# Two squares ahead of the first SiLU, one store per query part, late w_out pieces and the quotient at other blocks, the prompt's sums on VectorE

## The chip, the core and the metric

The kernel runs on one core of a Trainium2 chip. A core has TensorE (PE, the matrix engine; its weight loads are listed as PEld), VectorE (DVE), ScalarE (ACT), GpSimd (POOL) and SyncE (SP). Each engine works through its own instructions in order and waits on semaphores for the others. SP computes nothing; here it issues most of the DMAs, and ACT issues the rest. A DMA that has to wait for something holds up all that stands behind it in the same queue. The metric is the time of one execution on the device in microseconds (us).

## What is computed

One layer of a diffusion step: 128 context ("prompt") tokens and 1024 latent tokens, width 1024, with one combined input projection for two groups of heads, A (mixer 0, all latent keys) and B (mixer 1, a window of 128 to each side, with a sink logit). Cut to what matters:

```python
shift, scale, gate = modulation(cond, w_mod, b_mod)          # silu(cond) @ w_mod + b_mod
h = rmsnorm(x, norm_gain) * (1.0 + scale) + shift
q_a, k_a, v_a, g_a, q_b, k_b, v_b, g_b = project(h, w_in, qn_a, kn_a, qn_b, kn_b)
# latent tokens: q and k through apply_rope
o_a = softmax(q_a @ [k_ctx, k_lat].T / 8) @ [v_ctx, v_lat]
o_b = softmax([sink, q_b @ [k_ctx, k_band].T / 8])[1:] @ [v_ctx, v_band]
x = x + gate * (concat(o_a * silu(g_a), o_b * silu(g_b)) @ w_out)
# the prompt attends to its own keys alone; its k and v are outputs too
```

Everything is float32. To keep the precision, the kernel splits an operand into a high and a low part and adds two or three matmuls.

## The kernel before, in words

There are nine tiles of 128 tokens: `t` = 0 is the prompt, 1 to 8 are the latent tiles. The order of the instructions on every engine is that of the program text (`in_order`). A step is put off with `later(n, f)`: `f` runs `n` ticks on, and `block` (L276) ticks twice per projection block, the attention loop (L1309) once per slot.

*Start (L342 to L567).* SP loads latent tiles 1 to 4 and then, piece by piece, the modulation weights `wm` and the first columns of `w_in`. ACT loads the condition vectors `colt` and takes their SiLU (L375). `norm(t)` (L413) then takes the squares of a tile with their sum on ACT, the mean on POOL (L419), and a power of -0.5 on POOL (L421); `scaled` (L410) multiplies the tile on DVE. `turned` (L427) transposes a block of it on TensorE. Between the four transposes TensorE runs `warm(n)` (L461), matmuls whose results are not used, by the list `WARM`. After the fourth transpose come the modulation of the first block (`modulate_rows`, L387) and the matmuls of the first gates.

*Queries (L615 to L726).* For each mixer `m` and tile `t`, TensorE projects the queries; `query` (L650) normalizes, rotates and transposes them. `turned` (L683) copies the high part out of PSUM on ACT (L689), `low` (L693) takes the low part on DVE (L694), and `put` (L697) stores each part to DRAM in two DMAs, one for each half of the partitions, into `q_dram`, an array of 128 rows x 1024. The last three tiles of mixer 1 (`LAST_QUERIES`) are stored by SP, the others by ACT. The buffers of a part are two. After the queries SP loads the key tables `kcos` and `ksin` (L777), into memory that the queries used, and the keys are made (`key`, L819; `put_keys`, L779; transposes at L791, low parts at L809).

*Attention (L1131 to L1329).* The work is cut into 36 units (t, m, g), g being a half of the heads; the four prompt units come last. A unit of mixer 0 has 9 key blocks (1 for the prompt), one of mixer 1 three or four, and each block is a slot. In a slot TensorE makes the scores of this block (L1164 and L1165 for mixer 0, L1159 for mixer 1), and three slots later (`LAG`) it multiplies with the values (L1185 to L1188). The scores L1165 need `qb`, loaded by SP (L927) and completed by DVE (L942). `u_load` (L898) loads a unit's queries. After a unit's last block its end is spread over the next slots by `END_AT` = (1, 4, 6, 9): `inverse` on ACT (L1197 or L1199), `gated` on DVE and POOL (L1209, L1211), `parts` (L1221, L1223), and the output projection (L1256). The accumulator `pv` has two buffers, so the values of unit i + 2 wait for `gated` of unit i.

For mixer 1, `weight_items` (L951) makes the softmax: `ex` (L1001), its exponential (L1012), the sum (L1015) and its reciprocal (L1018). The prompt's four heads are then multiplied by it on DVE (L1021).

Five pieces of `w_out` (11 to 15) are loaded late, at the slots that `WO_LATE` gives, into a tag of two buffers (`yt`), and are split three slots later (L1078 on ACT, L1079 on POOL). The last piece of the gates is turned into a SiLU by way of exponentials and a logarithm (`put_quotient`, L302), at ticks that `QUOTIENT_AT` sets.

Of the kernel before, what the change touches and what calls it, by code (L numbers as in the profile page):

```python
# [49 lines left out]
QUOTIENT_AT = 9  # L50
# [3 lines left out]
WO_LATE = {12: 18, 13: 19, 11: 20, 14: 30, 15: 31}  # L54
# [7 lines left out]
WARM = (7, 4, 5, 4, 2, 8)  # L62
# [10 lines left out]
END_AT = (1, 4, 6, 9)  # L73
PROMPT_END = (2, 4, 5, 7)
# [7 lines left out]
LAST_QUERIES = ((1, 7), (1, 8), (1, 0))  # L82
CACHE_AT = 8
# [30 lines left out]
def hybrid_step(ctx, tc, x_prompt, x_sample, cache_k_a, cache_v_a, cache_k_b, cache_v_b,  # L114
# [9 lines left out]
    q_dram = [[dram.tile([P, 1024], F32, name=f"qd{t}_{m}") for m in range(2)] for t in range(NT)]  # L124
# [218 lines left out]
    with tc.tile_pool(name="st", bufs=2, side="right") as st:  # L343
# [6 lines left out]
        nc.scalar.dma_start(colt, cols)  # L350
        st.tile([P, 16], F32, name="pad3", bufs=1)
# [32 lines left out]
        nc.vector.tensor_copy(sil32[:, :, 0:2], sil2)  # L384
# [28 lines left out]
        def norm(t, now_=True):  # L413
            xm = xn[t]
            sq = st.tile([P, D], BF16, tag="sq", name=f"sq{t}", bufs=1)
            ss = st.tile([P, 1], F32, tag="ss", name=f"ss{t}")
            nc.scalar.activation(sq, xm, AF.Square, accum_out=ss)
            ms = st.tile([P, 1], F32, tag="ms", name=f"msx{t}")
            nc.gpsimd.tensor_scalar(ms, ss, 1.0 / D, EPS, op0=ALU.mult, op1=ALU.add)  # L419
            r = st.tile([P, 1], F32, tag="rs", name=f"rsx{t}")  # L420
            nc.gpsimd.tensor_tensor(r, ms, mhalf[:, 0:1], op=ALU.pow)  # L421
            if now_:
                scaled(t, r)
            else:
                rx[t] = r
# [59 lines left out]
        for j in range(KT + 2):  # L485
            if j == 0:
                px = bank_tr("px0_1")
                for i in range(4):
                    norm(1 + i)
                    warm(WARM[i])  # L490
                    turned(px[:, P * i : P * i + P], 0, 1 + i)
                modulate_rows(0)
                W_GA.split()
                warm(WARM[4])
                modulate(0)
                modulated(px, 0, 1, 4, 0)
                warm(WARM[5])
                continue
# [3 lines left out]
            if j == 1:  # L502
                load_wm(3)
                norm(5, False)
# [15 lines left out]
            if j == 1:  # L520
# [3 lines left out]
                norm(6, False)  # L524
# [27 lines left out]
            if X_FROM < j <= X_FROM + 3:  # L552
                norm(rest[j - X_FROM - 1], False)
# [61 lines left out]
    with tc.tile_pool(name="qt", bufs=2, side="right") as qt:  # L615
# [34 lines left out]
        def query(pq, m, t, tabs, n=1):  # L650
# [32 lines left out]
            def turned():  # L683
# [7 lines left out]
                (later if (m, t) not in ((1, 0), (1, 5)) else at_once)(1, lambda: low(ptq, qo))  # L691

            def low(ptq, qo):  # L693
                nc.vector.tensor_tensor(qo[1], ptq, qo[0], op=ALU.subtract)  # L694
                (later if (m, t) != (1, 0) else at_once)(1, lambda: put(qo[1], 1))

            def put(part, i):  # L697
                for g in range(2):
                    (nc.sync if (m, t) in LAST_QUERIES else nc.scalar).dma_start(q_dram[t][m][64 * i : 64 * i + 64, 512 * g : 512 * g + 512],
                                       part[64 * g : 64 * g + 64].bitcast(F32))  # L700
# [197 lines left out]
    def u_load(i):  # L898
# [3 lines left out]
        nc.sync.dma_start(qt_.bitcast(F32), q_dram[t][m][:, 512 * g : 512 * g + 512])  # L902
        qtile[i] = qt_

    def max_items(i):
# [19 lines left out]
        def finish():  # L925
            qb_ = qp.tile([68, 512], F32R, tag="qb", name=f"qb{i}", bufs=2)
            nc.sync.dma_start(qb_[0:64, :].bitcast(F32), q_dram[t][m][0:64, 512 * g : 512 * g + 512])  # L927
# [23 lines left out]
    def weight_items(i):  # L951
# [48 lines left out]
        def finish():  # L1000
            nc.gpsimd.tensor_tensor(v["ex"], v["nm"], sink[:, 4 * g : 4 * g + 4], op=ALU.add)  # L1001
# [12 lines left out]
        def total():  # L1014
            nc.gpsimd.tensor_tensor(v["sum"], v["sum"], v["ex"], op=ALU.add)  # L1015
# [162 lines left out]
    def values(i, b, last, blk, ph, pl):  # L1178
# [46 lines left out]
        ends = END_AT if t else PROMPT_END  # L1225
# [167 lines left out]
```

## Time and profile before

| | us |
|---|---|
| three runs | 720.32, 720.82, 721.16 (median 720.82) |
| the profiled execution | 720.69 |
| its span, first to last instruction | 718.9 |
| TensorE busy | 698.7 (97%) |
| DVE, ACT, POOL busy | 454.2, 413.9, 338.3 |
| mean granted TensorE clock | 0.995 |

In a row of the timeline the columns are start, length, engine, line, operation, output <- inputs, shapes and count, and in brackets the engine's idle time before it and what ended it; SPq and ACTq are DMA issues. A row of waits is: who waited, for what, us in total, how many times, the longest. A row of windows has the stretch, its length, the busy time of PE, PEld, DVE, ACT and POOL (with the number of instructions), the granted TensorE clock, the share of the DMA engines and GB/s. A row of a line or tile gives the shortest, median and longest duration in ns, and the first and last start in us.

### The profile page before, as it was taken

What the parts mean: (1) busy time and instruction counts of PE and PEld (TensorE: products, weight loads), DVE (VectorE), ACT (ScalarE), POOL (GpSimd) and SP (SyncE); (2) the same over time, 40 slices, a digit from 0 to 9 for tenths busy, and PEclk for the clock granted to TensorE, in tenths of its full rate; (3) what the DMA queues carried; (4) which work ended last, traced back from release to release, by engine and by line L of the source; (5) the groups of instructions that cost most, each with busy time, mean ns of one, the idle gap of its engine ahead of it and who ended that gap; (6) DMA issues with size and microseconds to landing.
All of it is one profiled execution on the core that took longest, in us unless ns stands there. A gap on an engine that the chain in (4) does not pass through costs nothing.

```text
span 718.9 us, 10656 instructions
## 1 busy us (share of the span) xinstructions
PE 698.7 (97%) x3530; PEld 559.1 (78%) x3530; DVE 454.2 (63%) x1002; ACT 413.9 (58%) x835; POOL 338.3 (47%) x357
## 2 busy tenths in 40 slices
PE   6999999999999999999899999999999999999987
PEld 2678988877787889976688888888888888887765
DVE  3575247866757853567566677567676775676552
ACT  4546411412323441188678877887788778877850
POOL 3466023232313330255767554755575557556660
PEclk9999999999999999999999999999999999999999
DMA  9951273348445025422132122121221221222223
GB/s 350 385 195 68 107 297 76 84 127 263 107 93 149 2 73 185 148 66 86 52 103 63 48 67 89 45 81 58 83 73 39 72 82 46 81 69 71 89 81 118
DMA packets 53304, 78.57 MB, mean 109 GB/s; under 512 B 6585, under 2 KB 25465, under 8 KB 52353
## 3 DMA queue, kind: packets, MB, share of 16 engines
q1 hardware_dynamic: 45888, 67.70, 28.7%
q10 hardware_dynamic: 7360, 10.19, 5.3%
q8 instruction: 28, 0.46, 0.3%
q14 instruction: 28, 0.22, 0.1%
HBM read 58.69 MB, written 19.18 MB: 108 GB/s over the span
## 4 chain that ended last, share of the span: by engine, by line
PE 87%; DVE 5%; issue 2%; POOL 1%; ACT 1%; DMA 1%; SPq 1%; ACTq 0%; DVEq 0%; POOLq 0%
PE po L1256 13%; PE pv L1185 6%; PE pv L1188 6%; PE pmx L922 5%; PE st L1164 5%; PE st L1165 5%; PE pv L1187 5%; PE pq L257 4%; PE pq L258 4%; PE pq L259 4%; PE st L1159 4%; PE pg L271 3%; PE pg L272 3%; PE pg L267 3%; PE sn L979 2%; PE sn L980 2%
## 5 line engine op out<-in xcount | busy, mean ns | idle before, releaser
L1175 POOL TENSOR_TENSOR pl<-pe,ph 128x512 fp32r<-128x512 f32 x130 | 167.6, 1291 | 150.3 <-DVE nm L983 65.9
L923 DVE TENSOR_REDUCE mx<-pmx 128x1 f32<-128x384 f32 x192 | 101.0, 552 | 59.9 <-PE pmx L922 58.7
L1167 ACT ACTIVATE pe<-st 128x512 f32<-128x512 f32 x146 | 86.9, 596 | 29.7 <-PE st L1165 28.9
L1171 ACT CAST ph<-pe 128x512 fp32r<-128x512 f32 x146 | 90.6, 620 | 4.8
L1185 PE MATMUL pv<-ph,v_hi 128*128 128x512 f32 x208 | 83.0, 399 | 2.3 <-DVE spare L1209 2.3
L1188 PE MATMUL pv<-pl,v_hi 128*128 128x512 f32 x208 | 82.8, 398 | 0.0
L1256 PE MATMUL po<-wo,ogh 128*128 128x512 f32 x216 | 74.0, 399 | 0.2 <-DVE yt L1265 0.2
L182 POOL TENSOR_TENSOR rs_q<-ms_q,mhalf 128x8 f32<-128x8 f32 x18 | 34.8, 1931 | 81.8 <-DVE ms_q L180 81.8
L983 DVE CUSTOM_DVE_ANT_0 sn<-sn,mask,nsink 128x512 f32<-128x512 f32 (+1 forms) x64 | 46.4, 725 | 40.5 <-PE sn L980 37.6
L922 PE MATMUL pmx<-kha,qt 128*128 128x384 f32 x192 | 61.5, 367 | 0.3 <-DVE mx L923 0.2
L1165 PE MATMUL st<-qb,kla 68*128 68x512 f32 x144 | 57.6, 400 | 2.8 <-DMA qb<-qd 2.8
L1164 PE MATMUL st<-qt,kha 128*128 128x512 f32 x144 | 57.7, 401 | 0.9 <-DVE pl L1161 0.9
L1187 PE MATMUL pv<-ph,v_lo 128*64 128x512 f32 x146 | 57.8, 396 | 0.0
L1188 PEld LDWEIGHTS pv<-pl,v_hi 128*128 128x128 f32 x208 | 39.6, 190 | 17.1 <-POOL pl L1175 0.7
L969 ACT ACTIVATE pen<-sn,nm 128x512 f32<-128x512 f32 (+2 forms) x72 | 45.1, 628 | 6.1 <-DVE nm L996 2.7
L1185 PEld LDWEIGHTS pv<-ph,v_hi 128*128 128x128 f32 x208 | 39.5, 190 | 10.4 <-ACT ogh L1221 2.1
L1160 ACT CAST ph<-st 128x512 fp32r<-128x512 f32 x62 | 36.4, 587 | 18.2 <-PE st L1159 17.6
L1256 PEld LDWEIGHTS po<-wo,ogh 128*128 128x128 f32 x216 | 40.6, 191 | 7.2 <-DVE yt L1265 0.6
L1161 DVE TENSOR_TENSOR pl<-st,ph 128x512 fp32r<-128x512 f32 x62 | 42.4, 685 | 4.7 <-ACT ph L1160 4.1
L1256 PE MATMUL po<-wo,ogl 128*128 128x512 f32 x108 | 42.8, 397 | 0.0
L922 PEld LDWEIGHTS pmx<-kha,qt 128*128 128x128 f32 x192 | 35.5, 190 | 8.3 <-DVE mx L923 2.8
L658 ACT ACTIVATE sqq<-pq 128x512 f32<-128x512 f32 x18 | 10.8, 599 | 53.1 <-DMA qd<-qo0q 15.2
(227 smaller groups left out, 1702.1 us busy)
## 6 DMA issues: line engine op xcount, KB each, us to landing
qt<-qd SPq DMA_DIRECT2D x36, 256.0 KB, 2.9
wm<-in_w_mod_ss_dram SPq DMA_DIRECT2D x7, 1024.0 KB, 7.7
sgl<-gd SPq DMA_DIRECT2D x36, 128.0 KB, 2.2
out_dram<-yt SPq DMA_DIRECT2D x17, 256.0 KB, 2.1
xn<-in_x_sample_dram SPq DMA_DIRECT2D x8, 512.0 KB, 7.7
wg<-in_w_mod_g_dram SPq DMA_DIRECT2D x4, 1024.0 KB
wraw<-in_w_out_dram SPq DMA_DIRECT2D x16, 256.0 KB, 3.6
yt<-in_x_sample_dram SPq DMA_DIRECT2D x16, 256.0 KB, 3.0
```

The source lines that it names most:

```text
L922: nc.tensor.matmul(pm[:, 0:384], lhs, kha[:, g, 3 * b : 3 * b + 3, :], start=True, stop=True)
L923: nc.vector.tensor_reduce(mx[:, h, b : b + 1], pm[:, 0:384], axis=AX.X, op=ALU.max)
L983: nc.vector.tensor_tensor_reduce(s, s, mask[:, m0 : m0 + n], -1.0, nsink[:, 4 * g + h : 4 * g + h + 1], op0=ALU.add, op1=ALU.min, accum_ou ...
L1164: nc.tensor.matmul(s, kh, qtile[i], start=True, stop=False)
L1165: nc.tensor.matmul(s, kl, qbtile[i], start=False, stop=True)
L1167: nc.scalar.activation(pe, s, AF.Exp)
L1171: nc.scalar.copy(ph, pe)
L1175: nc.gpsimd.tensor_tensor(pl, pe, ph, op=ALU.subtract)
L1185: nc.tensor.matmul(pv, two, ph, start=(b == 0), stop=False)
L1187: nc.tensor.matmul(pv[0:64, :], vl, ph, start=False, stop=False)
L1188: nc.tensor.matmul(pv, two, pl, start=False, stop=last)
L1256: nc.tensor.matmul(po[n], a, wo_parts[KT * n + k][lo], start=(k == KS[0] and p == 0), stop=(k == KS[-1] and p == 2))
```

## The change

1. Start: the table of functions is loaded by an instruction of its own; squares and means of tiles 1 and 2 are issued ahead of the SiLU and what follows it (`conditions`), those of tiles 3 and 4 one tile ahead; the means of tiles 1 to 4 are taken on DVE; the warming matmuls are (4, 3, 3, 5, 2, 7) instead of (7, 4, 5, 4, 2, 8).
2. Queries: `q_dram` has 256 rows x 512, the high part in the first 128 and the low part behind them; `put` stores a part in one DMA, and `u_load` reads a unit in two. Of the last three tiles SP stores the low parts alone. The low parts of tile 8 are taken at once, tile 5 and the prompt as before, and those of tiles 7 and 8 are stored at once.
3. `WO_LATE`: piece 11 at slot 30 instead of 20, 14 at 31 instead of 30, 15 at 33 instead of 31.
4. `QUOTIENT_AT` is 8 instead of 9.
5. `EDGE_END`: for mixer 0 of the first and the last latent tile `gated` comes three instead of four slots after the end.
6. For the prompt `ex` and the sum are on DVE instead of POOL.

```diff
-QUOTIENT_AT = 9
+QUOTIENT_AT = 8
-WO_LATE = {12: 18, 13: 19, 11: 20, 14: 30, 15: 31}
+WO_LATE = {12: 18, 13: 19, 11: 30, 14: 31, 15: 33}
-WARM = (7, 4, 5, 4, 2, 8)
+WARM = (4, 3, 3, 5, 2, 7)
+EDGE_END = (1, 3, 6, 9)
+AT_ONCE = ((1, 5), (1, 8), (1, 0))
-    q_dram = [[dram.tile([P, 1024], F32, name=f"qd{t}_{m}") for m in range(2)] for t in range(NT)]
+    q_dram = [[dram.tile([2 * P, 512], F32, name=f"qd{t}_{m}") for m in range(2)] for t in range(NT)]
...
         nc.scalar.dma_start(colt, cols)
+        nc.scalar.add_instruction(mybir.InstLoadActFuncSet(
+            name=nc.get_next_instruction_name(), engine=mybir.EngineType.Activation, act_func_set_id=18))
...
-        nc.scalar.activation(silc, colt[:, 0:16], AF.Silu)
-        nc.vector.tensor_scalar(bsc1, colt[:, 32:40], 1.0, None, op0=ALU.add)
-        nc.vector.tensor_copy(sil32[:, :, 0:2], sil2)
+        def conditions():
+            nc.scalar.activation(silc, colt[:, 0:16], AF.Silu)
+            nc.vector.tensor_scalar(bsc1, colt[:, 32:40], 1.0, None, op0=ALU.add)
+            nc.vector.tensor_copy(sil32[:, :, 0:2], sil2)
...
-        def norm(t, now_=True):
+        def norm(t, eng=nc.gpsimd):
...
-            nc.gpsimd.tensor_scalar(ms, ss, 1.0 / D, EPS, op0=ALU.mult, op1=ALU.add)
+            eng.tensor_scalar(ms, ss, 1.0 / D, EPS, op0=ALU.mult, op1=ALU.add)
...
-            if now_:
-                scaled(t, r)
-            else:
-                rx[t] = r
+            rx[t] = r
...
                 px = bank_tr("px0_1")
+                norm(1, nc.vector)
+                norm(2, nc.vector)
+                conditions()
                 for i in range(4):
-                    norm(1 + i)
+                    if 0 < i < 3:
+                        norm(2 + i, nc.vector)
+                    scaled(1 + i, rx.pop(1 + i))
                     warm(WARM[i])
...
-                (later if (m, t) not in ((1, 0), (1, 5)) else at_once)(1, lambda: low(ptq, qo))
+                (at_once if (m, t) in AT_ONCE else later)(1, lambda: low(ptq, qo))
...
-                (later if (m, t) != (1, 0) else at_once)(1, lambda: put(qo[1], 1))
+                (at_once if (m, t) in LAST_QUERIES else later)(1, lambda: put(qo[1], 1))
...
-                for g in range(2):
-                    (nc.sync if (m, t) in LAST_QUERIES else nc.scalar).dma_start(q_dram[t][m][64 * i : 64 * i + 64, 512 * g : 512 * g + 512],
-                                       part[64 * g : 64 * g + 64].bitcast(F32))
+                eng = nc.sync if i and (m, t) in LAST_QUERIES else nc.scalar
+                eng.dma_start(q_dram[t][m][P * i : P * i + P, :], part.bitcast(F32))
...
-        nc.sync.dma_start(qt_.bitcast(F32), q_dram[t][m][:, 512 * g : 512 * g + 512])
+        for s in range(2):
+            r0 = P * s + HD * g
+            nc.sync.dma_start(qt_[HD * s : HD * s + HD].bitcast(F32), q_dram[t][m][r0 : r0 + HD, :])
...
-            nc.gpsimd.tensor_tensor(v["ex"], v["nm"], sink[:, 4 * g : 4 * g + 4], op=ALU.add)
+            (nc.gpsimd if t else nc.vector).tensor_tensor(v["ex"], v["nm"], sink[:, 4 * g : 4 * g + 4], op=ALU.add)
...
-            nc.gpsimd.tensor_tensor(v["sum"], v["sum"], v["ex"], op=ALU.add)
+            (nc.gpsimd if t else nc.vector).tensor_tensor(v["sum"], v["sum"], v["ex"], op=ALU.add)
...
-        ends = END_AT if t else PROMPT_END
+        ends = (EDGE_END if m == 0 and t in (1, NL) else END_AT) if t else PROMPT_END
```

More of the change, by code (lines that the diff above doesn't have):

```diff
@@ L503, in hybrid_step @@
                 load_wm(3)
-                norm(5, False)
+                norm(5)
             if big_on:
@@ L523, in hybrid_step @@
                 transposed(1, 1, 4, 0)
-                norm(6, False)
+                norm(6)
                 first_gates(2, 0)
@@ L552, in hybrid_step @@
             if X_FROM < j <= X_FROM + 3:
-                norm(rest[j - X_FROM - 1], False)
+                norm(rest[j - X_FROM - 1])
             for ch in range(4):
@@ L926, in finish @@
             qb_ = qp.tile([68, 512], F32R, tag="qb", name=f"qb{i}", bufs=2)
[L927 removed]
+            nc.sync.dma_start(qb_[0:HD, :].bitcast(F32), q_dram[t][m][HD * g : HD * g + HD, :])
             qbtile[i] = qb_
```

## The prediction

> **What bounds the kernel now.** I read the page first, then the waits of TensorE, then the busy time in single windows of 3.41 us, and last the timelines around each wait.
>
> ```profile
> span 718.9 us, 10656 instructions
> ```
> ```profile
> PE st L1165 <- DMA qb<-qd: 2.8, 1, 2.8
> PE pv L1185 <- DVE spare L1209: 2.3, 4, 0.9
> PE px L428 <- DVE xn L411: 1.7, 4, 0.6
> PE ptk L791 <- DVE klp L809: 1.4, 1, 1.4
> PE st L1164 <- DVE pl L1161: 0.9, 1, 0.9
> ```
>
> The profiled execution took 720.69 us, 1.8 over its span, and the median of the runs is 720.82; I sum against 720.69. TensorE hardly ever stops: between its first and its last matmul these five waits are nearly all its idle time, 9.1 us. So no edit pays by making another engine faster; it pays by ending one of these waits, or by starting the chain of matmuls earlier. I take the parts by wait.
>
> One more loss is in no list of waits: the clock.
>
> ```profile
> 4.79:8.20 3.41, 2.92 (x7) 0.89 (x7) 0.78 (x4) 2.19 (x4) 1.04 (x4) 1.00 1.04 403
> 230.06:233.48 3.42, 1.99 (x12) 1.44 (x11) 3.30 (x13) 2.34 (x8) 0.71 (x3) 1.00 0.72 232
> 346.12:349.53 3.41, 0.97 (x5) 0.37 (x2) 0.83 (x2) 0.19 (x1) 2.16 (x3) 1.00 0.42 118
> 349.53:352.94 3.41, 3.08 (x7) 2.48 (x8) 1.51 (x3) 3.24 (x6) 1.28 (x1) 0.50 0.20 46
> 690.86:694.27 3.41, 1.76 (x9) 1.20 (x9) 2.01 (x6) 2.37 (x5) 2.93 (x4) 1.00 0.06 17
> 694.27:697.68 3.41, 3.22 (x8) 1.98 (x7) 1.73 (x5) 2.44 (x6) 2.47 (x4) 0.50 0.24 70
> ```
>
> The second column is the window's length, the next TensorE's busy time, and the 0.50 the granted clock. Two windows ran at half clock, and just before each lies a window in which TensorE was busy for only 0.97 and 1.76 us of 3.41. A window with 1.99 us (230.06) was followed by none. I read this as: a window that is too empty costs the next one half its clock. So two of the waits cost more than their length.
>
> **The change part by part. Start.** Two squares go ahead of the SiLU, the means of tiles 1 to 4 from POOL to DVE.
>
> ```profile
> L417 ACT ACTIVATE sq<-xn x4: 1039/1056/1057, 6.1 to 9.7; 128x1024 bf16<-128x1024 f32 x4
> L417 ACT ACTIVATION_READ_ACCUMULATOR sq<-xn x4: 186/186/186, 7.0 to 10.7; 128x1 f32 x4
> L411 DVE TENSOR_SCALAR xn<-xn,rsx x4: 754/754/754, 8.2 to 12.6; 128x1024 f32<-128x1024 f32 x4
> ```
> ```profile
> DMA to landing us min/median/max: 4.6/5.0/5.4
> ```
> ```profile
> 9.08 0.56 POOL L421 TENSOR_TENSOR rsx<-msx,mhalf 128x1 f32<-128x1 f32 x1
> 9.73 0.75 POOL L419 TENSOR_SCALAR msx<-ss 128x1 f32<-128x1 f32 x1
> ```
> ```profile
> 5.28 3.11 PE L464 MATMUL pg_s<-ident_b 128*128 128x512 bf16 x7 [5.28 <-DVE ident_b L347]
> 9.01 0.33 PE L428 MATMUL px<-ident,xn 128*128 128x128 f32 x1 [0.62 <-DVE xn L411]
> 9.17 1.03 PE L464 MATMUL pg_s<-ident_b 128*128 128x512 bf16 x4
> ```
>
> The landing times are those of tiles 2 and 3, issued at 1.2 and 1.6: they landed at 5.8 and 7.0, one tile in 1.3 us, so tile 1 was there at about 4.5 and its square waited behind the SiLU until 6.1. A square with its readout takes 1.23. After the change: square 1 from 4.5 to 5.7, square 2 from 5.8 to 7.05, the small SiLU, squares 3 and 4 done at 8.5 and 9.75. DVE scales tile 1 behind the SiLU's copy, from 7.4; tile 2 from 8.65 behind mean 3; tile 3 from 9.9 behind mean 4. POOL's mean of 0.75 us ran just beside a scaling of 0.75: POOL is held while DVE scales. So power 4, issued at 10.0, waits until 10.65, takes 0.55, and tile 4 is scaled from 11.2 to 11.95. Its transpose comes at 12.0, where it came at 12.6 + 0.75 = 13.4: 1.4 us earlier, if TensorE is free. The first seven warming matmuls went at 0.43 a piece, the next at 0.22: until 8.2 TensorE ran at half clock, whatever the 1.00 of that window says. Of the seven only four are left, 1.9 us of busy time in the first window, about the 1.76 that was too little. I take it that TensorE stays slow until the next boundary, 11.6: transposes 1 to 3 with three matmuls of 0.43 behind each reach 11.6, five more at 0.22 end at 12.8. Gain **0.6**, with 1.4 (clock full at 8.2) and -0.6 (slow until 15) as bounds. The 24 matmuls instead of 30 cost nothing else. What follows is bound by TensorE and moves up as a whole; the 1 MB of modulation weights that come behind tile 4 need 2.6 us at the 403 GB/s of the window, so they are there at about 11, an estimate, and hold up nothing.
>
> **Stores of the queries.** One store in place of two.
>
> ```profile
> 213.36 4.85 SPq L699 DMA_DIRECT2D qd<-qo1q  x6
> 218.26 0.59 SPq L777 DMA_DIRECT2D kcos<-in_k_cos_dram  x1
> ```
> ```profile
> 216.41 0.69 DVE L694 TENSOR_TENSOR qo1q<-ptq,qo0q 128x512 fp32r<-128x512 f32 x1 [4.32 <-DMA qd<-qo1q]
> ```
> ```profile
> 220.29 0.37 ACT L816 CAST v_hi<-pk 128x256 fp32r<-128x256 f32 x1 [8.65 <-DMA qd<-qo1q]
> ```
>
> At the end of the queries twelve stores stand on SP, 0.6 us each; the last low part waits 4.32 us for a buffer that a store still reads, the key tables are loaded behind all of them, and ACT waits for the last store to land. After the change SP issues three stores, the first parts go to ACT (three more issues of 0.6 there, while it was idle for 8.65), and each low part is stored at once. The last of the six ended its issue at 213.36 + 4.85 = 218.2; I count the last of three at 213 to 215, and so the keys 3 to 5 us earlier. The wait of 1.4 at L791 ends 12 us later in a chain of DVE work that begins with these keys: all **1.4** go, since 3 us cover it. Elsewhere the halved issues free ACT, but TensorE waits for nothing there: 0. The second q load of each unit puts one more issue of at most 0.6 on SP in a stretch where SP mostly waits: 0 (the price without that cover is the third rival).
>
> **Late w_out pieces.**
>
> ```profile
> 340.56 0.38 SPq L1145 DMA_DIRECT2D sgl<-gd  x1
> 346.39 0.33 SPq L1062 DMA_DIRECT2D wraw<-in_w_out_dram  x1
> 347.15 0.48 SPq L927 DMA_DIRECT2D qb<-qd  x1
> ```
> ```profile
> SPq L1062 <- POOL wo_big L1079: 5.4, 1, 5.4
> ```
> ```profile
> 349.34 0.62 ACT L1078 CAST wo<-wraw 128x512 fp32r<-128x512 f32 x1 [4.94 <-DMA wraw<-in_w_out_dram]
> ```
>
> Piece 11's load stood 5.4 us on SP until POOL had freed its buffer, and unit 4's `qb` load, next in the queue, went out at 347.15, for a matmul that then waited for it. Without the piece `qb` goes out behind the gate load of 340.56, some 6 us earlier, and ACT has no cast to wait for. The **2.8** us of the list go. Next late is ACT's cast of slot 23, which stood behind piece 11's; with ACT free for those 4.94 us it has time in hand. Window 346.12 is then full, so by my reading 349.53 keeps its clock: seven matmuls at 0.43 instead of 0.23, **1.4**.
>
> The wait comes back in part. Piece 15 is now loaded at slot 33 into piece 11's buffer, which is split in that same slot.
>
> ```profile
> 370.35 1.28 POOL L1079 TENSOR_TENSOR wo_big<-wraw,wo_big 128x512 fp32r<-128x512 f32 x1
> ```
> ```profile
> 371.38 0.47 SPq L927 DMA_DIRECT2D qb<-qd  x1
> ```
> ```profile
> 373.97 0.59 ACT L1199 ACTIVATE rs<-pv 64x512 f32<-64x512 f32 x1 [0.86 <-PE pv L1188]
> ```
>
> The split of slot 33 ended on POOL at 371.63, so the load goes out there, and unit 6's `qb` behind it about 1 us later than at 371.38. The piece lands near 374.6 and its cast stands on ACT ahead of L1199, which started at 373.97: ACT is 1.2 us late, and the scores two slots on may wait. I take **-0.6**, between 0 and -1.3.
>
> **Quotient, EDGE_END.** The quotient's steps leave slots 8 to 11 for 7 to 10, ahead of the DVE work that L1164 waits for 0.9 us. They run before it in either order, so only gaps that they now fill are gained: **0.2** (0 to 0.9). Gating one slot earlier for the units at the edges ends the first of the four waits of L1185, 2.3 - 1.8 = 0.5, of which I take **0.4**; the other three lie at the prompt, from 680 to 700:
>
> ```profile
> PE pv L1185 <- DVE spare L1209: 1.8, 3, 0.9
> ```
>
> **Prompt's sums on DVE.**
>
> ```profile
> 689.12 0.20 POOL L1001 TENSOR_TENSOR ex<-nm,sink 128x4 f32<-128x4 f32 x1
> 689.64 0.20 POOL L1015 TENSOR_TENSOR sum<-sum,ex 128x4 f32<-128x4 f32 x1 [0.32 <-ACT ex L1012]
> ```
> ```profile
> 689.88 0.18 DVE L1018 RECIPROCAL inv<-sum 128x4 f32<-128x4 f32 x1 [2.27 <-POOL sum L1015]
> ```
>
> POOL comes to the prompt's `ex` only at 689.12, and DVE stands 2.27 us for the sum. DVE was idle from 687.6, so with both sums there the reciprocal could follow at 687.6 + (689.88 - 689.12) = 688.4, or 1.5 earlier; ACT still has exponentials ahead, so I take 1.1, and 0.2 us of DVE for each sum lies in time that was idle. The three waits of 1.8 shrink by **1.1** (0.5 to 1.8); the rest is the chain of ACT and DVE behind. Window 690.86 then has some 2.8 us of work, and 694.27 keeps its clock: five matmuls at 0.2, **1.0**.
>
> The sum: 0.6 + 1.4 + 2.8 + 1.4 - 0.6 + 0.2 + 0.4 + 1.1 + 1.0 = 8.3, so 720.7 - 8.3 = **712.4 us**.
>
> By the Trainium skill, TensorE: Matmul & The Clock Gate, Part 1 and "HAM oscillation", the clock falls after an idle window of some 3.4 us, and the rule it draws is to leave no idle gap longer than that. The trace agrees on the window's length, but its longest gap after the start is 2.8; by that rule the two slow windows have another cause and stay, and the sum is 2.4 smaller, 714.8. Which it is, this trace cannot settle.
>
> **Rivals.** (1) *The slow windows stay.* They begin 344.7 us apart, which fits a schedule as well as two empty windows; but both follow the two emptiest ones. Then 2.4 less: 714.8 us. (2) *The wait moves.* If piece 15 holds up unit 6 as piece 11 did unit 4, a wait of 2.8 and a slow window of 1.4 are paid again, in place of my 0.6: 716.0. Against it: ACT and `qb` had time in hand here. (3) *Slower: the second q load makes `qb` late in every unit.*
>
> ```profile
> 395.23 0.47 SPq L927 DMA_DIRECT2D qb<-qd  x1
> ```
> ```profile
> 399.76 0.40 PE L1165 MATMUL st<-qb,kla 68*128 68x512 f32 x1
> ```
> ```profile
> qb<-qd SPq DMA_DIRECT2D x18, 128.0 KB, 2.9
> ```
>
> `qb` lands 1.6 us before its use. A delay beyond that is paid in 16 units; from 2.1 us on it eats the whole gain, and at 2.5 the time is 712.4 + 16 x 0.9 = 726.8. One issue of 0.6 speaks against it. (4) *It does little:* the start stays slow to 15 us and the key wait and the tail find new releasers: 720.
>
> **How the numbers follow.** Forecast 0.5, with a start at full clock (711.6) in it; slow windows stay 0.24; moved wait 0.14; little 0.07; slower 0.05. Low end: start 0.8 better, no loss at slot 33, the whole 1.8 of the tail: 712.4 - 2.1 = 710.3, and I go to 709.8. The high end takes in both middle rivals: 716.2. A difference of 0.2% (1.4 us) is about what can be told from none; faster 0.89, same 0.06, slower 0.05.
>
> **What would show it.** Start: transpose 4 before 13.4, warming matmuls at 0.43 up to about 11.6. Keys: no wait at L791, ACT's L816 before 217. Late pieces: no wait of L1165 and no clock of 0.50 after it; a short wait in unit 6. Tail: L1018 about 1 us behind the last exponential, L1185 waiting for less than 0.8 in all. I am wrong if a half-clock window stays without an empty window before it, or if `qb` shows up among the waits of many units.

## The result, and the profile after

| | before | after |
|---|---|---|
| median of four runs, us | 720.99 (720.32 to 721.24) | 711.64 (711.54 to 712.52) |
| the profiled execution, us | 720.69 | 711.62 |

The ratio is 0.9874, with a 95% interval from 0.9857 to 0.9892: 9.3 us less, where 8.3 were forecast. The page of the changed kernel opens so:

```profile
span 709.8 us, 10658 instructions
```

The waits of TensorE in the changed kernel follow. Its lines stand some ten further down: L1174 and L1175 are the scores that were L1164 and L1165, L1195 the values that were L1185, L432 the first transposes. `sn` are the scores of mixer 1, `pmx` products from which the row maxima of a coming unit are taken:

```profile
PE px L432 <- DVE xn L418: 1.6, 2, 1.1
PE pv L1195 <- DVE spare L1219: 1.5, 2, 0.8
PE st L1174 <- DVE pl L1171: 0.8, 2, 0.4
PE sn L989 <- ACT spare L1045: 0.4, 1, 0.4
PE pmx L932 <- ACT pen L979: 0.3, 1, 0.3
```

Two of the five waits that carried the prediction are gone: `qb` (2.8) and the key transposes (1.4). The values at the prompt wait twice instead of three times. New are two small ones, of `sn` and of `pmx`, and the 0.9 of the scores is now two waits of 0.4, one of them in a place where none was. From 12.21 us on, no window of the changed kernel ran at half clock until the work was done. These are the windows at the places of the two stalls:

```profile
344.56:347.97 3.41, 3.41 (x16) 2.81 (x15) 1.94 (x6) 3.27 (x7) 1.96 (x2) 1.00 0.04 13
684.64:688.06 3.42, 1.97 (x9) 1.12 (x8) 2.36 (x5) 2.68 (x6) 2.45 (x5) 1.00 0.17 50
```

To see where the 9 us come from, compare the start of the same matmul in both profiles. First some rows of before, then those of after:

```profile
13.43 0.33 PE L428 MATMUL px<-ident,xn 128*128 128x128 f32 x1 [0.28 <-DVE xn L411]
...
232.63 0.63 PE L791 MATMUL ptk<-ident_r,k2k 128*128 128x128 f32 x4 [1.44 <-DVE klp L809]
...
346.67 0.43 PE L1164 MATMUL st<-qt,kha 128*128 128x512 f32 x1
349.86 0.79 PE L1165 MATMUL st<-qb,kla 68*128 68x512 f32 x1 [2.77 <-DMA qb<-qd]
...
353.21 0.39 PE L1164 MATMUL st<-qt,kha 128*128 128x512 f32 x1
...
377.53 0.39 PE L1164 MATMUL st<-qt,kha 128*128 128x512 f32 x1
...
691.88 0.47 PE L1185 MATMUL pv<-ph,v_hi 128*128 128x512 f32 x1 [0.86 <-DVE spare L1209]
```
```profile
12.93 0.27 PE L432 MATMUL px<-ident,xn 128*128 128x128 f32 x1
...
229.41 0.60 PE L799 MATMUL ptk<-ident_r,k2k 128*128 128x128 f32 x4
...
343.57 0.44 PE L1174 MATMUL st<-qt,kha 128*128 128x512 f32 x1
343.85 0.39 PE L1175 MATMUL st<-qb,kla 68*128 68x512 f32 x1
...
345.71 0.39 PE L1174 MATMUL st<-qt,kha 128*128 128x512 f32 x1
...
370.58 0.47 PE L1174 MATMUL st<-qt,kha 128*128 128x512 f32 x1 [0.40 <-DVE pl L1171]
...
683.85 0.40 PE L1195 MATMUL pv<-ph,v_hi 128*128 128x512 f32 x1
```

The distance of two such starts is the gain so far, and the growth of it from row to row is what the stretch between them gave:

| up to | gain so far | this stretch | forecast for it |
|---|---|---|---|
| fourth transpose | 0.50 | 0.50 | 0.6 (start) |
| key transposes | 3.22 | 2.72 | 1.4 (stores) |
| unit 4, first scores | 3.10 | -0.12 | 0.6 (quotient 0.2, EDGE_END 0.4) |
| unit 4, scores with `qb` | 6.01 | 2.91 | 2.8 (piece 11) |
| end of the former half-clock window | 7.50 | 1.49 | 1.4 |
| unit 6, the slot of the late piece | 6.95 | -0.55 | -0.6 |
| prompt, first values that waited | 8.03 | 1.08 | 1.1 (prompt's sums) |
| end of the span (718.9 - 709.8) | 9.1 | 1.1 | 1.0 (half-clock window) |

Six of eight stretches came out within 0.15 of their term. The stores gave twice theirs (1.3 more), and the quotient with EDGE_END gave nothing (0.7 less): the two misses cancel in part. Whether each stretch belongs to the edit that I put beside it, this table cannot tell; the experiments can.

### The profile page after: what moved, and what is told of

It is laid out like the page before. It is cut to its first block, busy times and chain, and to the rows that moved or that the text cites. A ratio compares the mean times of both kernels' runs of the same rounds, so it can differ in the third digit from the quotient of the medians.

```text
span 709.8 us, 10658 instructions
## 1 busy us (share of the span) xinstructions
PE 694.6 (98%) x3524; PEld 557.6 (79%) x3524; DVE 454.4 (64%) x1010; ACT 414.0 (58%) x835; POOL 335.7 (47%) x349
## 5 line engine op out<-in xcount | busy, mean ns | idle before, releaser
L1185 POOL TENSOR_TENSOR pl<-pe,ph 128x512 fp32r<-128x512 f32 x130 | 167.5, 1291 | 149.7 <-ACT ph L1181 70.2
L1195 PE MATMUL pv<-ph,v_hi 128*128 128x512 f32 x208 | 82.5, 397 | 1.5 <-DVE spare L1219 1.5
L1174 PE MATMUL st<-qt,kha 128*128 128x512 f32 x144 | 57.9, 402 | 0.8 <-DVE pl L1171 0.8
L1175 PE MATMUL st<-qb,kla 68*128 68x512 f32 x144 | 57.0, 396 | 0.0
L698 ACT CAST qo0q<-ptq 128x512 fp32r<-128x512 f32 x18 | 10.6, 587 | 65.8 <-PE ptq L695 59.9
L1195 PEld LDWEIGHTS pv<-ph,v_hi 128*128 128x128 f32 x208 | 39.3, 189 | 8.5 <-ACT ogh L1231 1.1
```

What stands on the lines that cost most here:

```text
L1174: nc.tensor.matmul(s, kh, qtile[i], start=True, stop=False)
L1175: nc.tensor.matmul(s, kl, qbtile[i], start=False, stop=True)
L1185: nc.gpsimd.tensor_tensor(pl, pe, ph, op=ALU.subtract)
L1195: nc.tensor.matmul(pv, two, ph, start=(b == 0), stop=False)
```

## The experiments

### Each part alone

Five kernels are the kernel before with one part of the change. The first takes the start (the hunks of the first part of the change, and `WARM`):

```diff
-WARM = (7, 4, 5, 4, 2, 8)
+WARM = (4, 3, 3, 5, 2, 7)
...
+                norm(1, nc.vector)
+                norm(2, nc.vector)
+                conditions()
```

> The kernel before with the start of the change alone (squares of tiles 1 and 2 first, means on DVE, warming matmuls 4, 3, 3, 5, 2, 7). My theory: TensorE stays slow to the second window boundary, near 12, and the fourth transpose comes near 12.9 where it came at 13.43; all that follows moves up by 0.5 to 0.6, so about 720.4 against 721.0, ratio 0.999. The other end, clock full from the first boundary: 1.4 less, ratio 0.998. Rival (the gain is lost before the first gates): 0. Both half-clock windows, near 349 and 694, stay in either case by my theory of the empty window, for both stalls stay; by the rival schedule they stay too, so this run does not tell these apart.

Measured: 720.54 against 720.89 us, ratio 0.9998 (0.9987 to 1.0008). In its profile, the window ahead of the first boundary, the one that the stall of unit 4 empties (behind it the clock was at 0.50), and the one at the prompt:

```profile
6.09:9.50 3.41, 2.46 (x7) 0.58 (x6) 1.88 (x6) 2.88 (x6) 1.60 (x3) 1.00 1.05 340
347.42:350.84 3.42, 1.27 (x6) 1.06 (x7) 0.55 (x1) 1.66 (x3) 1.48 (x2) 1.00 0.27 90
692.17:695.58 3.41, 2.00 (x10) 1.09 (x8) 2.36 (x5) 2.58 (x6) 2.10 (x3) 1.00 0.13 38
```

The gain is too small for these runs, and the profile says why. The windows do not begin at the same time in every execution: a boundary lay at 8.20 in the profile of before and lies at 9.50 here. Where the window ahead of it was too empty (2.46 us), TensorE stays slow for one more window, here to 12.92, and the fourth transpose came at 13.14. Against 13.43 that is 0.3. So the start's worth depends on where the boundary falls. At the prompt the first two waits are nearly those of before (0.94 and 0.79, where before has 0.86 and 0.80). The fullness of the window differs with the boundary, 2.00 us of matmuls where before had 1.76, and no half-clock window followed: from 691.9 in before to the last matmuls this kernel gained 0.9, though its part of the change does not touch the prompt.

The second takes the stores:

```diff
-                for g in range(2):
-                    (nc.sync if (m, t) in LAST_QUERIES else nc.scalar).dma_start(q_dram[t][m][64 * i : 64 * i + 64, 512 * g : 512 * g + 512],
-                                       part[64 * g : 64 * g + 64].bitcast(F32))
+                eng = nc.sync if i and (m, t) in LAST_QUERIES else nc.scalar
+                eng.dma_start(q_dram[t][m][P * i : P * i + P, :], part.bitcast(F32))
```

> The kernel before with the stores of the queries alone (one store per part, two loads per unit, low parts of tile 8 at once). My theory: the keys' tables are loaded 3 to 5 us earlier, the wait of 1.4 at the low parts of the keys goes, time falls by 1.4 (in the profile of the changed kernel the same stretch gained 2.1, some of which may come from smaller waits near 224). Ratio 0.998 to 0.997. Rival (the second load makes qb late): a wait on qb in several units and slower by up to 6. Rival (little): the wait moves to the next releaser and the time stays.

Measured: 717.76 against 720.89 us, ratio 0.9959 (0.9947 to 0.9972), 3.0 us less. The two transposes of the keys at L791, from its timeline:

```profile
223.37 0.60 PE L791 MATMUL ptk<-ident_r,k2k 128*128 128x128 f32 x4
...
229.81 0.60 PE L791 MATMUL ptk<-ident_r,k2k 128*128 128x128 f32 x4
```

SP loads the key tables at 212.28 instead of 218.26, and ACT stands 2.97 us for the stores instead of 8.65. In before the same two transposes had a wait each, the larger of which I had counted (1.44, above), and the smaller not:

```profile
224.58 0.66 PE L791 MATMUL ptk<-ident_r,k2k 128*128 128x128 f32 x4 [0.28 <-ACT k2k L785]
```

Both are gone. This kernel's fourth transpose, in a start that wasn't changed, came at 13.29, 0.14 ahead of that of before. So the part itself gave, up to here, 232.63 - 229.81 - 0.14 = 2.68 in this profile: 224.58 - 223.37 - 0.14 = 1.07 up to the first of the two transposes, and 1.61 from there to the second. No wait on `qb` appears beyond the one of 2.7 in unit 4. Its half-clock windows:

```profile
343.07:346.48 3.41, 1.35 (x6) 0.69 (x4) 1.17 (x3) 0.00 (x0) 2.52 (x3) 1.00 0.38 118
346.48:349.90 3.42, 2.80 (x7) 2.22 (x8) 1.51 (x3) 3.25 (x6) 1.28 (x1) 0.50 0.15 39
349.90:353.31 3.41, 3.41 (x10) 2.64 (x9) 0.68 (x2) 2.19 (x5) 1.49 (x2) 0.50 0.27 76
```

Here two windows in a row ran at half clock: the first of them, with 2.80 us of matmuls, was not full enough to raise the clock again.

The third is `WO_LATE` alone:

```diff
-WO_LATE = {12: 18, 13: 19, 11: 20, 14: 30, 15: 31}
+WO_LATE = {12: 18, 13: 19, 11: 30, 14: 31, 15: 33}
```

> The kernel before with the late w_out pieces alone (11 at slot 30, 14 at 31, 15 at 33). Theory of the empty window: the wait of 2.8 on qb goes, and with it the half-clock window behind it (1.4 to 1.5), less 0.4 to 0.6 for the piece at slot 33: 3.6 to 3.9 less, about 717.2, ratio 0.995; the other half-clock window, at the prompt, stays, near 690.5. Rival schedule: the wait goes and a half-clock window stays near 349 (or 345 us ahead of the second), 2.2 to 2.4 less, about 718.7.

Measured: 716.10 against 720.89 us, ratio 0.9935 (0.9920 to 0.9950), 4.7 less. The windows at the places of the two stalls:

```profile
347.57:350.98 3.41, 3.41 (x16) 2.73 (x16) 1.82 (x5) 3.27 (x7) 2.17 (x3) 1.00 0.37 103
688.91:692.32 3.41, 2.11 (x10) 1.15 (x9) 2.33 (x5) 2.69 (x6) 2.22 (x4) 1.00 0.14 38
```

The wait on `qb` is gone and the clock is full there: the schedule would have kept a slow window. The price came too, a wait of 0.52 for `pl` at 374.55, in unit 6. It is also full at the prompt, where I expected the slow window to stay, since the sums there are unchanged: the boundary fell so that the emptiest window held 2.11. That is why the part gave more than its 3.7.

The fourth has the prompt's sums on DVE alone:

```diff
-            nc.gpsimd.tensor_tensor(v["ex"], v["nm"], sink[:, 4 * g : 4 * g + 4], op=ALU.add)
+            (nc.gpsimd if t else nc.vector).tensor_tensor(v["ex"], v["nm"], sink[:, 4 * g : 4 * g + 4], op=ALU.add)
```

> The kernel before with the prompt's two sums on DVE alone. Theory of the empty window: the three waits of 1.8 at the prompt shrink by 1.1, the window before 694 then has 2.8 us of matmuls and the half-clock window behind it goes, 1.0: 2.1 less, about 718.9, ratio 0.997, and the half-clock window near 349 stays. Rival schedule: the waits shrink by 1.1, a half-clock window stays near 694: 1.1 less, about 719.9. Rival (another releaser ends the waits just as late): 0.

Measured: 719.51 against 720.89 us, ratio 0.9987 (0.9974 to 0.9999). The waits from 680 to 700:

```profile
PE pv L1185 <- DVE spare L1209: 1.5, 2, 0.8
```

One of three waits is gone, the 0.86 at 691.88; the other two are 0.79 and 0.68. In before they are 0.80 and 0.19, but there the third comes after the slow window; in the first and the third experiment, which had no slow window there, it is 0.68 and 0.69. So 0.9, not 1.1 spread over three, plus the half-clock window only in those executions that had one. By the ratio it is 0.9, with an interval from 0.1 to 1.9: that takes in the 1.1 of the rival and leaves out the 2.1 that I expected. Nor does this profile's full clock at the prompt tell the two apart, for the first three experiments show it there with the old sums. The theory of the empty window rests on the other experiments.

The fifth takes `QUOTIENT_AT` and `EDGE_END`:

```diff
-QUOTIENT_AT = 9
+QUOTIENT_AT = 8
-        ends = END_AT if t else PROMPT_END
+        ends = (EDGE_END if m == 0 and t in (1, NL) else END_AT) if t else PROMPT_END
```

> The kernel before with the quotient's ticks at 8 and the earlier gating of the edge units alone. My theory: the wait of L1185 on the gating of the first unit, 0.5, goes, and the wait of 0.9 of L1164 shrinks by some 0.2: 0.6 less, 720.4, ratio 0.999. The changed kernel's profile shows gains of 0.5 each at 326 and 332, but also small new waits of 0.9 in all from 334 to 338; if those belong to this part, it is worth 0 to 0.2. The half-clock windows stay by both theories.

Measured: 719.50 against 720.17 us, ratio 0.9994 (0.9979 to 1.0009). Its waits from 300 to 345, and one row at the prompt:

```profile
PE st L1165 <- DVE pl L1162: 0.4, 1, 0.4
PE sn L980 <- ACT spare L1036: 0.3, 1, 0.3
PE pmx L923 <- ACT pen L970: 0.3, 1, 0.3
```
```profile
691.33 0.47 PE L1186 MATMUL pv<-ph,v_hi 128*128 128x512 f32 x1 [0.25 <-DVE spare L1210]
```

The wait on the first unit's gating went, as forecast, and the 0.9 of the scores became 0.4, more than forecast; but `sn` and `pmx` now wait for ACT, and give most of it back. ACT runs the same steps in the same order from 326 to 339 in both kernels, with no idle time of note but 0.31 us in before, so it could not follow what TensorE had gained: the same cast of `ph` starts at 333.88 in before and at 333.79 here. Another 0.3 went just before, where TensorE transposes the row maxima (at 323.97 in before): the quotient's product, moved up on DVE, now runs ahead of a step that makes them. The new waits are those of the changed kernel, so they belong to this part. And it does what I had not seen: gating one slot earlier for the last latent tile, next to the prompt, shortens the first wait at the prompt from 0.86 to 0.25, the same wait that the prompt's sums remove. The two parts share it.

By the ratios the five parts gave 0.1, 3.0, 4.7, 0.9 and 0.4 us of 721, 9.1 in all, against 9.1 for the whole. Each interval is 1.5 to 2.5 us wide from end to end, so this agreement does not show that the parts are independent; the 0.6 that two of them share at the prompt is too small to be seen in it.

### Is it the empty window?

The sixth kernel is the kernel before with eleven matmuls whose result is overwritten, in the stall of unit 4:

```diff
         kh, kl = blk[0]
+        if (i, b) == (4, 0):
+            for _ in range(11):
+                nc.tensor.matmul(s, ident_b, ident_b.unsqueeze(1).to_broadcast([P, 4, P]), start=True, stop=True)
         nc.tensor.matmul(s, kh, qtile[i], start=True, stop=False)
```

> The kernel before, with eleven matmuls whose result is overwritten (0.22 each, 2.4 us in all) put ahead of the first scores of unit 4, so that they run inside the wait of 2.8 on qb. The qb wait shrinks to about 0.4 and its end stays where it was, since the queue of SP sets it. Theory of the empty window: window 346 then has 3.4 of 3.41 us of matmuls and the next keeps its clock: 1.4 to 1.5 less, 719.5, ratio 0.998, though TensorE has more to do. Rival schedule: the half-clock window near 349 stays, time 721.0 or a little more. Rival (the clock falls through what follows the stall, such as many engines starting at once): stays too.

Measured: 718.58 against 720.17 us, ratio 0.9977 (0.9963 to 0.9990). TensorE and the windows in its profile:

```profile
346.63 2.55 PE L1166 MATMUL st<-ident_b 128*128 128x512 bf16 x11
...
349.98 0.50 PE L1168 MATMUL st<-qb,kla 68*128 68x512 f32 x1 [0.58 <-DMA qb<-qd]
```
```profile
348.08:351.50 3.42, 2.84 (x14) 1.73 (x12) 1.18 (x2) 2.26 (x4) 1.46 (x2) 1.00 0.26 85
351.50:354.91 3.41, 3.41 (x16) 2.79 (x15) 1.13 (x4) 3.27 (x8) 1.40 (x2) 1.00 0.33 102
689.70:693.11 3.41, 1.70 (x9) 1.20 (x9) 2.01 (x6) 2.36 (x5) 2.97 (x4) 1.00 0.06 17
693.11:696.52 3.41, 3.19 (x8) 2.02 (x7) 1.74 (x5) 2.40 (x6) 2.47 (x4) 0.50 0.25 72
```

The stall ends where it did (349.98, before 349.86), TensorE does 2.5 us more work, and the kernel is 1.6 us faster: the clock stays full behind the stall. Without the eleven, TensorE would have idled from 348.08 to 349.98, and this window would have held 351.50 - 349.98 = 1.5 us. In the same execution the window of 1.70 at the prompt, left as it was, cost the next one half its clock. That settles it against a schedule. It speaks against the last rival of the expectation too: ACT and DVE start behind the stall as they did (ACT's cast of the piece at 349.19 after 4.83 us without work, in before at 349.34 after 4.94), and the clock does not fall.

The seventh is the changed kernel with six stalls meant to be made by a later `qb`:

```diff
-            nc.sync.dma_start(qb_[0:HD, :].bitcast(F32), q_dram[t][m][HD * g : HD * g + HD, :])
+            fetch = lambda: nc.sync.dma_start(qb_[0:HD, :].bitcast(F32), q_dram[t][m][HD * g : HD * g + HD, :])
+            later(LATE_Q[i], fetch) if i in LATE_Q else fetch()
...
+LATE_Q = {8: 2, 12: 3, 16: 2, 20: 3, 24: 2, 28: 3}
```

> The changed kernel with the qb load of units 8, 16 and 24 issued two slots later, and of units 12, 20 and 28 three slots later. A slot is about 2.1 us, and qb had 1.8 in hand: stalls of some 2.4 and 4.5 us, 3 of each, 21 us in all. Theory of the empty window: wherever a window of 3.41 us holds less than about 1.9 us of matmuls the next one shows a clock of 0.50 and costs 1.4 to 1.7 more; up to 6 such windows, 732 + 4 to 9, about 736 to 741; stalls that are cut in two by a window boundary cost no clock. Rival schedule: at most two half-clock windows, some 345 us apart and not tied to the stalls, 732 to 735. Rival (only a window with no matmul at all costs clock): only the stalls of 4.5 can, none to three windows.

Measured: 715.61 us, 4.0 more than the changed kernel's 711.64. Its wait on `qb`:

```profile
PE st L1177 <- DMA qb<-qd: 3.2, 3, 1.1
```

A miss: two slots cost nothing and three slots 1.1 us each, so the stalls were too short to empty a window, and none ran at half clock. SP's order shows why. Put two slots down, the load of unit 8 still stands behind the same store `rd` and ahead of the same loads of `spare`: it was issued at 388.04, and at 388.43 in the changed kernel, where everything near it is 0.4 later as well. Put three slots down, the load of unit 12 falls behind the loads of `spare`, goes out at 438.82 instead of 436.16, and is late by more than the 1.6 us that `qb` has in hand. So the delay of a load is set here by what stands ahead of it in SP's order, not by slots. My rival of the second q load needed more than these 1.6 us of delay to cost anything; neither the second experiment nor the changed kernel shows a wait of that kind.

### Versions that might be faster

The eighth puts seven warming matmuls first in the changed kernel:

```diff
-WARM = (4, 3, 3, 5, 2, 7)
+WARM = (7, 3, 3, 5, 2, 7)
```

> The changed kernel with seven warming matmuls instead of four ahead of the first transpose. My reading of the start: the window that ended at 8.80 held 2.35 us of matmuls, and that was not enough to raise the clock; with seven at 0.43 it holds some 3.3, the clock is full from 8.8, the second to fourth transposes are bound by DVE (scaled tile 4 is ready at 11.70) and the fourth comes at 11.9 instead of 12.93: 0.9 to 1.0 less, about 710.7, ratio 0.986 against before. Rival (the matmuls after the start fill by time, not by activity): the clock still rises at 12.2, three more matmuls of 0.43 make the transposes 0.2 to 0.4 later: 711.9. Rival (the modulation weights land only near 13): the transposes are earlier, what follows is not: 711.6.

Measured: 710.84 us, ratio to before 0.9875 (0.9853 to 0.9897). The clock was full from 10.50 and the fourth transpose came at 12.15, 0.78 ahead of that of the changed kernel; the time is 0.80 less than its 711.64, in separate runs, and every one of the four runs is below every one of the other's. I had expected the full clock at 8.8; the boundary lay elsewhere, and the window ahead of 10.50 was full (3.41 us). With four warming matmuls and a lucky boundary three profiles have the fourth transpose about as early (12.12 to 12.40), so the profile alone does not show what the seven are worth; the times do.

The ninth moves piece 15 by a slot:

```diff
-WO_LATE = {12: 18, 13: 19, 11: 30, 14: 31, 15: 33}
+WO_LATE = {12: 18, 13: 19, 11: 30, 14: 31, 15: 34}
```

> The changed kernel with w_out piece 15 at slot 34 instead of 33. My theory: in the changed kernel the cast of piece 15 stands on ACT at 367.19 behind a wait of 1.59 for its DMA, and all that follows it on ACT (rs, then ph) is late, so that L1174 waits 0.4 at 370.58; one slot (2.1 us) later the cast has its data and lies behind rs and ph: that wait goes, 0.4 to 0.6 less than the changed kernel. Rival (the scores of the next slot wait in its place, 0.6 for a cast of 0.62): 0.

Measured: 710.88 us (four runs from 710.48 to 712.05), and 711.75 for the changed kernel run beside it (from 711.66 to 711.92). ACT in the changed kernel, and then in this one:

```profile
367.19 0.62 ACT L1088 CAST wo_big<-wraw 128x512 fp32r<-128x512 f32 x1 [1.59 <-DMA wraw<-in_w_out_dram]
367.84 0.60 ACT L1209 ACTIVATE rs<-pv 64x512 f32<-64x512 f32 x1
...
369.12 0.59 ACT L1170 CAST ph<-st 128x512 fp32r<-128x512 f32 x1
```
```profile
365.84 0.59 ACT L1209 ACTIVATE rs<-pv 64x512 f32<-64x512 f32 x1 [0.85 <-PE pv L1198]
...
367.12 0.59 ACT L1170 CAST ph<-st 128x512 fp32r<-128x512 f32 x1
367.61 0.62 ACT L1088 CAST wo_big<-wraw 128x512 fp32r<-128x512 f32 x1
```

In the first, the cast at the head of ACT's order waits 1.59 for its DMA, and `rs` and `ph` wait behind it; in the second it stands behind them and finds its data. The wait of 0.40 at 370.58 is gone. The two profiled executions, 710.48 and 711.74, differ by 1.26: 0.6 of it arises at that place in unit 6, and 0.6 at the fourth transpose, at 12.28 here and at 12.86 in the kernel beside it, which the edit does not touch. One of the four runs was slower than all of the kernel beside it, so the times alone do not show the gain; the rows show the mechanism.

The tenth takes the row sums of the prompt's units one slot earlier:

```diff
-PROMPT_END = (2, 4, 5, 7)
+PROMPT_END = (1, 4, 5, 7)
```

> The changed kernel with the row sums of the prompt's units (rs, ACT) one slot after their end instead of two. The two waits that are left at the prompt, 0.77 and 0.69 at 685.9 and 687.5, end with the gating on DVE, which had stood 1.33 us for rs on ACT. My theory: the chain of ACT and DVE sets them, and earlier rs take 0.5 to 1.2 off the two. Rival: ACT has no room earlier, so rs in front makes pe and ph as much later and the scores wait instead: 0 or slower by up to 0.6.

Measured: 716.27 us, 4.5 more than the 711.75 beside it, and far worse than either side had it. Two of its waits, a row of ACT, and its windows:

```profile
PE pv L1195 <- DVE spare L1219: 1.8, 1, 1.8
PE pv L1195 <- ACT ph L1181: 1.1, 1, 1.1
```
```profile
683.09 0.59 ACT L1209 ACTIVATE rs<-pv 64x512 f32<-64x512 f32 x1 [2.28 <-DVE spare L1219]
```
```profile
686.60:690.02 3.42, 1.16 (x4) 0.78 (x5) 1.53 (x3) 1.89 (x4) 2.47 (x5) 1.00 0.13 38
690.02:693.43 3.41, 3.41 (x10) 2.63 (x9) 1.19 (x3) 1.92 (x5) 3.07 (x5) 0.50 0.57 146
```

The direction is that of the rival: `rs` stands in front of `pe` and `ph`, and everything behind these is late. The size is not. `rs` has a single buffer, and at the head of ACT's order it stood 2.28 us until DVE's gating of the unit before was done; in the kernel beside it the same step finds no wait. The waits at the prompt grew from 1.5 to 3.5, and then the window held only 1.16 us of matmuls and a half-clock window came back, in a kernel that had none.

The last two are both gains together, and the changed kernel beside them:

```diff
-WO_LATE = {12: 18, 13: 19, 11: 30, 14: 31, 15: 33}
+WO_LATE = {12: 18, 13: 19, 11: 30, 14: 31, 15: 34}
-WARM = (4, 3, 3, 5, 2, 7)
+WARM = (7, 3, 3, 5, 2, 7)
```

> The changed kernel with seven warming matmuls first and w_out piece 15 at slot 34. My theory: both gains add, 0.6 to 0.9 from the start (0.8 between the medians of separate runs: 711.64 and 710.84) and 0.4 to 0.6 from the piece: 1.0 to 1.5 less than the changed kernel run beside it. Rival (the start's gain was scatter): 0.4 to 0.6. In the profile the clock is full at the first window boundary that ends a window with over 2.8 us of matmuls, at any phase at most 3.4 us after 8.5.

> The changed kernel once more, so that the three beside it have it on the same chip: ratio 0.987 to before, as in its first runs. The phase of the windows is free, so the clock at the start can be full anywhere from 8.5 to 15; theory of the empty window: no half-clock window unless one holds less than 1.9 us of matmuls, which only the two waits at the prompt (0.77 and 0.69, 0.9 apart) come near. Rival schedule: some half-clock window in mid-run.

Measured: 710.09 us (four runs from 709.91 to 710.15) against 711.75 (four from 711.66 to 711.92); the ratios to before are 0.9871 (0.9857 to 0.9885) and 0.9894 (0.9880 to 0.9908). TensorE at the start, with both:

```profile
5.35 3.17 PE L468 MATMUL pg_s<-ident_b 128*128 128x512 bf16 x7 [5.35 <-DVE ident_b L349]
...
11.96 0.28 PE L432 MATMUL px<-ident,xn 128*128 128x128 f32 x1
```
```profile
5.64:9.06 3.42, 3.42 (x10) 1.12 (x9) 1.66 (x7) 2.83 (x6) 1.60 (x3) 1.00 0.99 364
```

The seven fill the window, the clock is full from 9.06, and the fourth transpose comes at 11.96, 0.90 ahead of the 12.86 of the kernel beside it. The wait at unit 6 is the other part: the distance to the kernel beside it grows by 0.6 there. Together that is 1.5 of the 1.59 between the two profiled executions (710.15 and 711.74). This version beats both kernels: before by 1.3%, the changed one by 0.2%, with all four runs below its four. The clock of the changed kernel was full from 11.85 and stayed so to the end of its work, as in its first profile. Its time is that of its first runs, but on this chip the kernel before was faster (median 719.84), so the change gave 8.1 us here, where the first runs gave 9.3; the forecast of 8.3 lies between.

## Why the prediction was right

**The mechanism.** The time lay 0.8 below the forecast, in the case that I held likeliest. That it came so close is in part luck: the stores gave 1.3 more than their term and the quotient with EDGE_END 0.7 less. TensorE was the bound, its waits were the list to work from, and the clock was a second list: the windows that were too empty. The rival of slow windows on a schedule (714.8) fell with the late pieces alone and with the eleven matmuls. By the Trainium skill, TensorE: Matmul & The Clock Gate, Part 1 and "HAM oscillation", it takes an idle window of some 3.4 us to lose the clock. The runs disagree: in mid-run, windows with 0.67 to 1.76 us of matmuls lost it, with no idle stretch above 2.8. The measurement decides.

**Start, 0.6: right in size, by luck of the boundary.** I let TensorE stay slow until 11.6, and it did until 12.21. Two of my reasons held: ACT's squares come ahead of the SiLU, and four warming matmuls leave the window too empty (2.34). What I missed is that the boundary moves from one execution to the next. With the old start the fourth transpose came between 13.26 and 14.20 in six profiles, with the new one and four matmuls between 12.12 and 13.14 in six. The means, 13.5 and 12.6, make it 0.9. The times of the first experiment neither confirm nor exclude that: 0.1, with an interval from -0.6 to 0.9.

**Stores, 1.4: the mis-sized term, 2.7.** The wait at L791 was rightly traced to the stores on SP. The step that failed is "Elsewhere the halved issues free ACT, but TensorE waits for nothing there: 0". Ahead of it TensorE had lost another 1.1 us in pieces too small for my list of waits: one of 0.28 on the same line, and some of 0.12 and less. And a wait costs more than its length: the 1.44 gave 1.61. Of the terms, this one is the furthest off; less the 0.7 of the quotient, it leaves 0.6 of the distance of 0.8 to the forecast.

**Late pieces, 2.8 + 1.4 - 0.6: right in all three**, 2.91, 1.49 and -0.55. The rival in which piece 15 makes unit 6 wait as unit 4 did (716.0) had the right place and the wrong size: ACT and `qb` had the time in hand that I gave them.

**Quotient and EDGE_END, 0.6: wrong, -0.1.** Both waits shrank (0.9 to 0.4, more than I had taken, and 0.4 to none), but the gain was taken back: 0.3 by the quotient's product, which on DVE now runs ahead of a step that makes the row maxima, and the rest by ACT, which has hardly a pause from 326 to 339 and came only 0.1 earlier, so that `sn` and `pmx` waited. I had costed the moved steps at nothing without naming what stood behind them, and had not asked which engine would set the pace once the two waits were gone.

**Prompt's sums, 1.1 + 1.0: right in sum, for other reasons.** I spread 1.1 over three waits; one of 0.86 went, and two stayed: L1195 waits 1.5 in all, where I had named less than 0.8 as a sign. EDGE_END has a share in the same wait. The half-clock window behind is real and cost 0.9, as the first experiment shows where it was missing, but it is not in every execution: of the five kernels with the prompt as it was (before, and the first, second, third and sixth experiment) two show it. On an average of executions it is worth less than the 1.0, and that the profile of before had it is luck. I had put 2.8 us of matmuls into that window; in the changed kernel it held 1.97, little above the 1.92 that kept the clock elsewhere.

**What stays open.** The quotient and EDGE_END were not tried apart, and EDGE_END and the prompt's sums were not tried together without the rest. What the clock counts, busy time or something nearer to work done, is not settled either (below).

## What to carry to other kernels

When TensorE is busy 97% of the time, list its idle time twice: by what ended it, and by how full each window of 3.41 us was; a stall that empties a window costs a second time, 0.9 to 1.5 us here. Such a stall can be filled with matmuls that nobody needs, for a gain, if it can't be removed. Before moving a small step to an earlier slot, name what stands behind it on its engine, whether its buffer is free by then, and which engine sets the pace once the wait is gone: this lost the gain of one part here, and 4.5 us in the tenth experiment.

## What the runs showed of the hardware

**The windows run free.** They begin at another time in each execution: the boundary at which the clock was first full lay at 8.20 in before, 9.06, 11.06, 11.85 and 12.21 in others, up to 13.07 in the third experiment. (The Trainium skill, TensorE: Matmul & The Clock Gate, Part 1, says the same of the start of a kernel; these traces agree, and show it for stalls in mid-run too.) So the same stall costs a half-clock window in one execution and not in the next, when a boundary cuts it in two. Three runs of the kernel before even have a mean clock of 1.000, so that neither stall cost them a window (718.22 and 718.58 beside a median of 720.89, and 719.84 beside one of 719.84). The prompt's three waits left 1.70 to 2.11 us in their emptiest window, according to the boundary.

**There are two limits, and neither is one number.** In the middle of the 14 profiles, every window at full clock that held 0.67 to 1.76 us of matmuls was followed by half clock (eight of them), and every one with 1.92 or more by full clock. Once slow, a window with 2.80 was too little to come back and one with 3.08 enough; at the start 2.34, 2.46 and 2.66 were too little, and 2.72 and all above were enough (2.72 to 2.98 in six profiles), so less than the 2.80 that was too little in mid-run. The window in which the last matmul ends is another sample: seven that held 0.31 to 1.40 took the clock down, and one that held 1.64, in the combined kernel, did not:

```profile
701.96:705.37 3.41, 1.64 (x8) 1.02 (x6) 2.61 (x5) 0.00 (x0) 0.72 (x1) 1.00 0.20 77
```

The window behind it, empty, was at 1.00, and only the next at 0.50. Here 1.64 was enough, where 1.70 and 1.76 were not at the prompt. At the end of the work the matmuls lie close together, at the prompt they stand between waits, and one that stands alone looks longer (0.47 against 0.40 in the rows above). So the clock may count work done rather than busy time; no run here tells these apart.
